# A hybrid decoder layer on one core: one column tile of the merge gates taken out of the block products, and the order of splits, weight rounding and squares changed around the output projection

## The chip, the cores and the metric

The kernel runs on one core of one Trainium2 chip. The metric is the device time of one execution in microseconds (us). Each kernel is executed several times and its time is the median of those executions; one further execution is taken by the hardware profiler, and every row that is read here comes from that one. The engines are named as in the profile: PE is the matrix engine (PEld its weight loads), DVE the vector engine, ACT the scalar engine, POOL the general engine, SP the queue that issues most DMAs.

## What is computed

One layer of a decoder, for 512 tokens of width 1024, in float32. The part that the change touches is the mixer sublayer and the start of the memory sublayer:

```
h    = rms_norm(x) * gain
proj = h @ w_in          # q | k | v | u | B | C | g_a | g_b
o_a  = stick_breaking_attention(q, k, v)          # 8 heads of 64
y_b  = B * causal_conv3(C * u)
merged = sigmoid(g_a) * (o_a @ w_branch_a) + sigmoid(g_b) * (y_b @ w_branch_b)
x    = x + merged @ w_mix_out
x    = x + memory_cross_attention(rms_norm(x), rms_norm(mem), ...)
x    = x + swiglu(rms_norm(x)) ;  out = rms_norm(x)
```

The gates g_a and g_b are 1024 columns each, so eight column tiles of 128 for each of them.

## The kernel before, in words

All activations are held transposed: 128 channels on the partitions, 512 tokens along the free dimension. Every float32 operand of a matmul is **split** into two parts of a shorter float32 format (fp32r): a rounded copy "hi", made by ACT, and the remainder "lo", made by DVE as a subtraction. A product is then three matmuls, hi by hi, hi by lo and lo by hi (`mm3`, lines 170 to 173).

**Plain products.** `load_w` (lines 146 to 168, over `load_hi`) loads 128 columns of a weight (512 KB) into one of four buffers named wr, rounds it on ACT (wh, L163) and subtracts on DVE (wl, L166). `project` and `gemm` make one column tile of h @ w_in from it with 8 x 3 matmuls 512 wide into a PSUM bank of the pool `pmm`, which has two banks (tag mm).

**Block products.** For the wide projections a scheme after Strassen is used: two column tiles and two halves of the tokens form a 2 x 2 block product that needs 7 products in place of 8. `ffn_load` (lines 691 to 710) brings one such pair of column tiles (ws, wg and a22; part of the sums of weights is made by a DMA from POOL that adds into ws, L704), `ffn_raw` and `ffn_form` (lines 708 to 738) make the remaining sums and the splits, and `product` (L747) runs 4 x 3 matmuls 256 wide for each of the 7. The products go to banks z, v and y; v lies in the pool of two banks, z has four banks, y two. `order` (lines 784 to 790) interleaves the 7 products of one pair with those of the next. The gates' pair number m is column tile m of g_a and of g_b.

**Order of the stages around the change.** After the attention, lines 831 to 841 make the gates of the first 3 column tiles by plain products (two of the three were begun within the attention, and one half of the third), squash them with a sigmoid (`squash`), and call `branch` (lines 794 to 804): two gemms of 12 matmuls, first over `yb`, then over `oT`, each followed by a multiplication of its PSUM bank with its gate (L801), and a sum of the two (L803) into one tile of `raw_m`. `gate_pair` reloads x (into wr buffers), scales it and makes the sums that the block products take as their activations (`pair_forms`, `sums_of`, L591 to L595). These lines are ordered by the scheduler of the framework.

Lines 877 to 930 are a **manual schedule**: PE, ACT and DVE each run their instructions exactly in the order in which the program states them; the DMA queues are not part of it. It has two parts. First the last 5 column tiles of the gates as block products, each followed by its `branch` when its seventh product is done; `merge` splits the tiles of `raw_m` into `merged` (L185 on ACT, L186 on DVE) somewhere between them. Then the output projection `mix`, which is `block` inside `residual` (lines 632 to 681): for each of 8 column tiles one gemm of 24 matmuls into a bank of the two-bank pool, then `finish`, which adds x (L659), scales it by the gain of the next norm (xr, L661), splits it and makes the block forms for the memory queries (`even_forms`, `odd_forms`, L601 to L621), squares x (L671 on ACT) and adds the square to a running sum (L674 on DVE). `mix_w(m)` loads and rounds the weight of column tile m two tiles ahead and puts its subtraction on a list, `late`; `catch_up` runs what is on the list. Ahead of the loop `mix_w` is called for tiles 0 and 1, at the products (last_m, 2) and (last_m, 5) of the gates, each time with `catch_up` right behind it. Squares of tiles 0 to 6 are added through `late`, so behind the addition of x of the next tile.

Lines 932 to 954 are the **memory queries**: 4 block pairs, 28 products, with ACT and DVE reading the banks and making the weights' forms six products ahead (`AHEAD`).

Of the kernel before, what the change touches and what calls it, by code (L numbers as in the profile page):

```python
# [9 lines left out]
F32R = mybir.dt.float32r  # L10
AF = mybir.ActivationFunctionType
ALU = mybir.AluOpType

P = 128
# [16 lines left out]
NT = (NF - HOLD - TURN) // 2  # L31
NB = D // (2 * P)
QM = NF + NB
GATES = 5
GM = QM + D // (2 * P)
GATE_AHEAD = 4
MEM_AT = (5, 7, 9, 11)
# [10 lines left out]
def hybrid_layer(ctx: ExitStack, tc: tile.TileContext, xT_d, memT_d, cols_d, wv_d, win_d,  # L48
# [27 lines left out]
    def f(ap):  # L76
        return ap.bitcast(F32)
# [67 lines left out]

    def load_w(src, cols=P):

        w, rest = load_hi(src, cols)
        rest()
        return w  # L150

    def load_hi(src, cols=P):

        k = D // cols
# [5 lines left out]
        hi = wpool.tile([P, k, cols], F32R, tag="wh", name=nm("wh"))  # L160
        lo = wpool.tile([P, k, cols], F32R, tag="wl", name=nm("wl"))
        h2, l2 = (t.rearrange("p k c -> p (k c)") for t in (hi, lo))
        after(nc.scalar.copy(h2, raw), lead[-1:])  # L163

        def rest():
            lows.append(nc.vector.tensor_tensor(out=l2, in0=raw, in1=f(h2), op=ALU.subtract))  # L166

        return (hi, lo), rest
# [458 lines left out]
    def listed(first, oh, ol, ch, cl, dh, dl):  # L627
        a, b = slice(0, HS), slice(HS, S)
        return [first, (oh[:, a], ol[:, a]), (ch[:, a], cl[:, a]), (dh[:, a], dl[:, a]),
                (ch[:, b], cl[:, b]), (dh[:, b], dl[:, b]), (oh[:, b], ol[:, b])]  # L630

    def residual(w_dram, act, old, gain):


        xn = []
        acc = tmp("acc")
        ps, w, even, late = {}, {}, {}, []

        def weight(m):
            w[m], rest = load_hi(w_dram[m])  # L640
            late.append(rest)

        def catch_up():
            while late:
                late.pop(0)()

        def block(m, k0, k1, bank=mmtile):
            if k0 == 0:
                if m not in w:
                    w[m] = load_w(w_dram[m])  # L650
                ps[m] = bank("r")
            for k in range(k0, k1):
                mm3(ps[m], (w[m][0][:, k, :], w[m][1][:, k, :]), act[k], k == 0, k == KD - 1)
            if k1 == KD:
                finish(m)

        def finish(m):
            xm = old[m]
            nc.vector.tensor_tensor(out=xm, in0=ps[m], in1=xm, op=ALU.add)  # L659
            raw = f(unit("xr"))  # L660
            nc.scalar.activation(raw, xm, AF.Copy, scale=gain[:, m:m + 1])  # L661
            catch_up()
            if m % 2:
                xn.append(odd_forms(*even.pop(m - 1), raw))
            else:
                even[m] = even_forms(raw)
            if m == 0:
                nc.scalar.activation(acc, xm, AF.Square)
            else:
                sq = tmp("sq")  # L670
                nc.scalar.activation(sq, xm, AF.Square)  # L671

                def add():
                    nc.vector.tensor_tensor(out=acc, in0=acc, in1=sq, op=ALU.add)  # L674

                if old is x1 and x_loads and m < KD - 1 and not om:
                    late.append(add)
                else:
                    add()

        return (old, xn, acc), block, weight, catch_up

    KP = KD // 2
    SCALED = 3
# [109 lines left out]
    def branch(m, sig, w, also=()):  # L794
        for j, a in ((1, yb), (0, oT)):
            ps = mmtile("br")
            gemm(ps, w, a, 4 * j)
            for g in also[j:j + 1]:
                g()
            with tc.high_priority(100):  # L800
                nc.vector.tensor_tensor(out=sig[j], in0=ps, in1=sig[j], op=ALU.mult)  # L801
# [75 lines left out]
    with tc.manual_schedule(engines={mybir.EngineType.PE, mybir.EngineType.Activation,  # L877
                                     mybir.EngineType.DVE}):
        wb, last_m = {}, GM + GATES - 1

        def merge(n):
            for _ in range(n):
                merged.append(split(raw_m[len(merged)], "m"))

        for n, (m, i) in enumerate(gs):
            product(bank_of(m, i), m, i)
            if i == 1 and m > GM:
                gate_second(m - 1)
            gate_reads(m, i)
            if (m, i) == (last_m, 4):  # L890
                gate_second(m)
            if n + GATE_AHEAD < len(gs):
                ffn_form(*gs[n + GATE_AHEAD])
            if n + GATE_AHEAD + SUM_AHEAD < len(gs):
                ffn_raw(*gs[n + GATE_AHEAD + SUM_AHEAD])
            if i == 3:
                wb[m] = load_w(wbr_d[KD - GATES + m - GM])
            if (m, i) in ((last_m, 2), (last_m, 5)):
                if i == 2:
                    mix_all, mix, mix_w, catch_up = residual(wmix_d, merged, x1, g_q)  # L900
                mix_w(i // 3)
                catch_up()
            if (m, i) == (last_m - 1, 6):
                merge(2)
            if i == 6:
                if m == last_m:
# [4 lines left out]
                branch(KD - GATES + m - GM, (b["g"], b["t"]), wb[m],  # L911
                       (lambda: None, lambda: merge(1)) if m == last_m else ())
                sigmoid = b["sigmoid"]
            if m == last_m and i in (1, 2, 3, 4):
                merge(1)
        merge(KD - len(merged))

        qs = order(QM, MH)
        for m in range(KD):
            mix(m, 0, KD - 1)  # L920
            if m + 2 < KD:
                mix_w(m + 2)
            mix(m, KD - 1, KD)
            for n in {2: range(4), 4: range(4, AHEAD + SUM_AHEAD)}.get(m, ()):
                ffn_raw(*qs[n], nc.gpsimd)
            for n in {5: (0,), 6: (2, 3, 4)}.get(m, ()):
                ffn_form(*qs[n])
        catch_up()
        ffn_form(*qs[5])
        x1, x1f, acc1 = mix_all  # L930

    with tc.manual_schedule(engines={mybir.EngineType.PE, mybir.EngineType.Activation,
                                     mybir.EngineType.DVE}):
        for n, (m, i) in enumerate(qs[:3] + [(QM + 1, 0)]):
            product(bank_of(m, i), m, i, range(KP - 1 - n // 3))
        for m, i in qs[:3]:
            product(bank_of(m, i, False), m, i, range(KP - 1, KP))
        mks = [mem_load(k2) for k2 in range(KD // 2)]
        for n, (m, i) in enumerate(qs):
            if (m, i) == (QM + 1, 0):  # L940
                product(bank_of(m, i, False), m, i, range(KP - 2, KP))
            elif n > 2:
                product(bank_of(m, i), m, i)
            if i == 1 and m > QM:
                second(m - 1)
            elif (m, i) == (QM + MH - 1, 5):
                second(m)
            reads(m, i)
# [424 lines left out]
```

## Time and profile before

| | before |
|---|---|
| median of the runs | 858.8 us (855.7, 858.8, 859.72) |
| profiled execution, its time | 857.22 us |
| span of its instructions | 855.3 us (1.9 us lie outside the span) |
| busy, PE / PEld / DVE / ACT / POOL | 842.0 / 763.4 / 675.7 / 484.6 / 84.1 us |
| mean granted PE clock | 0.997 |

A row of the timeline has the start in us from the span's start, the duration, the engine, the line of the kernel, the operation, the tile written and the tiles read, the shapes, a count, and in brackets the idle time of the engine just before it with what ended it. Matmuls are pipelined: each lasts longer than the distance to the next, so their pace is read from start to start. The view of waits gives, for each engine and line, what it waited for, the total in us, the number of times and the longest. The view of windows gives busy time of each engine in a stretch of the span, and the clock that PE was granted in it.

### The profile page before, as it was taken

To read this page: it belongs to the slowest core of one execution; us is meant where nothing else is said; L and a number is where in the kernel's file an instruction comes from. 1 tells how busy PE (TensorE), PEld (TensorE's weight loads), DVE (VectorE), ACT (ScalarE), POOL (GpSimd) and SP (SyncE) were. 2 spreads that over 40 slices of the span, in tenths; PEclk is the share of its full clock that TensorE was granted. 3 is DMA by queue.
4 is the path that set the end of the run, shared out by engine and by line. 5 is a ranking of instruction groups with operands and counts; after the bars stand their busy time and mean duration, and the time that the engine had idled before them with its cause. 6 is when DMAs were issued, how large, how long until landed. Compare 5 with 4: busy or idle time off the path is not lost.

```text
span 855.3 us, 14081 instructions
## 1 busy us (share of the span) xinstructions
PE 842.0 (98%) x5380; PEld 763.4 (89%) x5380; DVE 675.7 (79%) x1179; ACT 484.6 (57%) x873; POOL 84.1 (10%) x107
## 2 busy tenths in 40 slices
PE   9999999999999989999999999999999999999997
PEld 7878787888899978899988889999999999888997
DVE  9769889987866857878865789888888878966864
ACT  7556766676544535667654666555554456652345
POOL 1011112211010010000000011111111110010002
PEclk9999999999999999999999999999999999999999
DMA  8432232216583664466433437777767775462312
GB/s 296 129 118 79 95 104 80 90 50 199 158 194 102 234 152 108 133 157 226 136 100 98 104 82 173 196 186 188 181 175 184 188 192 171 133 153 65 97 42 99
DMA packets 51027, 120.76 MB, mean 141 GB/s; under 512 B 5136, under 2 KB 9232, under 8 KB 50960
## 3 DMA queue, kind: packets, MB, share of 16 engines
q1 hardware_dynamic: 41152, 101.23, 36.3%
q0 software_dynamic: 9520, 18.35, 13.1%
q8 instruction: 42, 0.69, 0.3%
q10 hardware_dynamic: 288, 0.29, 0.1%
q14 instruction: 25, 0.20, 0.1%
HBM read 116.68 MB, written 2.10 MB: 139 GB/s over the span
## 4 chain that ended last, share of the span: by engine, by line
PE 91%; DVE 3%; ACT 2%; DMA 2%; issue 1%; POOL 0%; DVEq 0%; ACTq 0%; POOLq 0%
PE z L747 23%; PE y L747 11%; PE v L747 6%; PE pr L171 5%; PE pr L172 5%; PE pr L173 5%; PE f L172 3%; PE f L173 3%; PE f L171 3%; PE r L171 3%; PE r L173 3%; PE r L172 3%; PE v L277 3%; PE z L449 1%; PE o L477 1%; DMA ws<-in_w_gates_dram 1%
## 5 line engine op out<-in xcount | busy, mean ns | idle before, releaser
L166 DVE TENSOR_TENSOR wl<-wr,wh 128x1024 fp32r<-128x1024 f32 x80 | 97.5, 1222 | 23.9 <-ACT wh L163 21.4
L163 ACT CAST wh<-wr 128x1024 fp32r<-128x1024 f32 x80 | 83.5, 1048 | 54.7 <-PE pr L172 12.0
L747 PE MATMUL z<-xdh,wf 128*128 128x256 f32 x560 | 110.9, 282 | 0.9 <-ACT sa L771 0.9
L747 PEld LDWEIGHTS z<-xdh,wf 128*128 128x128 f32 x560 | 91.0, 189 | 1.3 <-issue 1.1
L171 PE MATMUL pr<-xgh,wh 128*128 128x512 f32 x208 | 81.5, 392 | 0.0
L172 PE MATMUL pr<-xgl,wh 128*128 128x512 f32 x208 | 81.2, 390 | 0.0
L173 PE MATMUL pr<-xgh,wl 128*128 128x512 f32 x208 | 81.1, 390 | 0.0
L747 PE MATMUL z<-xdl,wf 128*128 128x256 f32 x280 | 78.8, 281 | 0.0
L738 DVE TENSOR_TENSOR wf<-s,wf 128x512 fp32r<-128x512 f32 x70 | 48.2, 689 | 27.2 <-ACT wf L737 26.2
L771 ACT COPY sa<-z 128x256 f32<-128x256 f32 x52 | 19.3, 372 | 82.4 <-PE z L747 82.3
L729 DVE TENSOR_TENSOR wf<-wg,wf 128x1024 fp32r<-128x1024 f32 x35 | 42.9, 1224 | 23.2 <-ACT wf L728 23.2
L737 ACT CAST wf<-s 128x512 fp32r<-128x512 f32 x70 | 43.6, 623 | 26.2 <-DVE s L715 16.7
L747 PE MATMUL z<-xch,wf 128*128 128x256 f32 x280 | 56.2, 283 | 0.0
L747 PE MATMUL y<-xch,wf 128*128 128x256 f32 x280 | 56.1, 282 | 0.0
L704 POOL DMA_DIRECT2D ws<-in_w_ffn_in_dram x22 | 26.5, 1203 | 300.4 <-DMA ws<-in_w_ffn_in_dram 156.8
L747 PEld LDWEIGHTS z<-xdl,wf 128*128 128x128 f32 x280 | 53.0, 189 | 0.2
L738 DVE TENSOR_TENSOR wf<-ws,wf 128x512 fp32r<-128x512 f32 x70 | 48.7, 695 | 2.6 <-ACT wf L737 2.4
L737 ACT CAST wf<-ws 128x512 fp32r<-128x512 f32 x70 | 43.0, 617 | 11.1 <-PE v L747 4.6
L171 PE MATMUL f<-acth,wh 128*128 128x512 f32 (+1 forms) x144 | 49.3, 342 | 0.0
L172 PE MATMUL f<-actl,wh 128*128 128x512 f32 (+1 forms) x144 | 49.2, 342 | 0.0
L173 PE MATMUL f<-acth,wl 128*128 128x512 f32 (+1 forms) x144 | 49.2, 342 | 0.0
L747 PE MATMUL v<-xoh,wf 128*128 128x256 f32 x240 | 48.6, 283 | 0.2 <-ACT xoh L611 0.2
(331 smaller groups left out, 2456.3 us busy)
## 6 DMA issues: line engine op xcount, KB each, us to landing
wr<-in_w_in_dram SPq DMA_DIRECT2D x26, 512.0 KB, 3.6
ws<-in_w_ffn_in_dram SPq DMA_DIRECT2D x22, 512.0 KB, 4.1
ws<-in_w_ffn_in_dram POOLq DMA_DIRECT2D x22, 512.0 KB, 5.8
wg<-in_w_ffn_in_dram SPq DMA_DIRECT2D x22, 512.0 KB, 4.5
wr<-in_w_ffn_out_dram SPq DMA_DIRECT2D x14, 512.0 KB, 3.5
a<-in_w_ffn_in_dram SPq DMA_DIRECT2D x22, 256.0 KB, 4.9
wr<-in_w_branch_dram SPq DMA_DIRECT2D x8, 512.0 KB, 3.7
wr<-in_w_mix_out_dram SPq DMA_DIRECT2D x8, 512.0 KB, 4.0
```

Source lines behind the costliest of these rows:

```text
L163: after(nc.scalar.copy(h2, raw), lead[-1:])
L166: lows.append(nc.vector.tensor_tensor(out=l2, in0=raw, in1=f(h2), op=ALU.subtract))
L171: nc.tensor.matmul(ps, a[0], b[0], start=start, stop=False, **kw)
L172: nc.tensor.matmul(ps, a[0], b[1], start=False, stop=False, **kw)
L173: nc.tensor.matmul(ps, a[1], b[0], start=False, stop=stop, **kw)
L277: nc.tensor.matmul(vps[t], xg[k][a][:, sl], wv[k][b], start=k == 0 and (a, b) == (0, 0), stop=k == KD - 1 and a == 1)
L704: nc.gpsimd.dma_start(s13, a[:, 0:4:3, :], accum_op=ALU.add)
L729: nc.vector.tensor_tensor(out=lo, in0=pair, in1=f(hi), op=ALU.subtract)
L737: nc.scalar.copy(hi, raw)
L738: nc.vector.tensor_tensor(out=lo, in0=raw, in1=f(hi), op=ALU.subtract)
L747: nc.tensor.matmul(ps[:, :HS], a, b, start=i < 3 and k == 0 and j == 0, stop=k == KP - 1 and j == 2, skip_group_check=True)
L771: nc.scalar.copy((s[:, :HS], None, None, s[:, HS:], t[:, :HS], t[:, :HS])[i], z)
```

## The change

1. `GATES` goes from 5 to 4: column tile 3 of both gates is made by plain products and its branch runs in the first loop (now 4 rounds, with the four `gate_pair` calls one in each); the block products of the gates are 4 pairs.
2. `load_hi` is cut into `load_raw` (the DMA) and `halves` (rounding, and the subtraction as a function to call later). Ahead of `mix`, tile 0's weight is rounded where it was, but its subtraction now waits until (last_m - 1, 6), behind the products of the last but one tile and ahead of its branch. Tile 1's weight is only loaded at (last_m, 5); it is rounded within the last branch, behind that branch's second multiplication, and subtracted when all merges are done.
3. In `branch` the multiplication L801 now stands ahead of the extra work `also`. The two merges that stood ahead of the last but one branch stand behind its two multiplications; the merge inside the last branch stands behind that branch's first multiplication.
4. In `residual`, squares of tiles 0 to 3 of the output projection stay as they were. Squares of tiles 4 to 7, with their additions, are put on a list `sums` and run after products 6, 9, 12 and 15 of the memory queries. The second user of `residual` (`om` not empty) squares and adds at once, as before.

```diff
-GATES = 5
+GATES = 4
...
-    def load_hi(src, cols=P):
+    def load_raw(src):
         raw = wpool.tile([P, D], F32, tag="wr", name=nm("wr"))
         i = nc.sync.dma_start(raw, src)
...
+        return raw
+
+    def halves(raw, k=KD):
+        hi, lo = (wpool.tile([P, k, D // k], F32R, tag=t, name=nm(t)) for t in ("wh", "wl"))
...
         def weight(m):
-            w[m], rest = load_hi(w_dram[m])
+            if m not in raw:
+                weight_raw(m)
+            w[m], rest = halves(raw.pop(m))
             late.append(rest)
...
-                if old is x1 and x_loads and m < KD - 1 and not om:
+                if m < LATE_SQUARES and not om:
                     late.append(add)
                 else:
                     add()
+            if m < LATE_SQUARES or om:
+                square()
+            else:
+                sums.append(square)
...
             gemm(ps, w, a, 4 * j)
+            with tc.high_priority(100):
+                nc.vector.tensor_tensor(out=sig[j], in0=ps, in1=sig[j], op=ALU.mult)
             for g in also[j:j + 1]:
                 g()
-            with tc.high_priority(100):
-                nc.vector.tensor_tensor(out=sig[j], in0=ps, in1=sig[j], op=ALU.mult)
...
-            if (m, i) in ((last_m, 2), (last_m, 5)):
-                if i == 2:
-                    mix_all, mix, mix_w, catch_up = residual(wmix_d, merged, x1, g_q)
-                mix_w(i // 3)
-                catch_up()
-            if (m, i) == (last_m - 1, 6):
-                merge(2)
+            if (m, i) == (last_m, 2):
+                mix_all, mix, mix_w, mix_raw, catch_up, sums = residual(wmix_d, merged, x1, g_q)
+                mix_w(0)
+            elif (m, i) == (last_m, 5):
+                mix_raw(1)
             if i == 6:
+                also = ()
+                if m == last_m - 1:
+                    catch_up()
+                    also = lambda: merge(1), lambda: merge(1)
+                elif m == last_m:
+                    also = lambda: mix_w(1), lambda: merge(1)
...
-                       (lambda: None, lambda: merge(1)) if m == last_m else ())
+                branch(KD - GATES + m - GM, (b["g"], b["t"]), wb[m], also)
...
         merge(KD - len(merged))
+        catch_up()
...
             if i == 6:
                 mem_split(mks[m - QM], m - QM)
+            if n in (6, 9, 12, 15):
+                sums.pop(0)()
```

`branch` runs its gemm over `yb` first, so `also[1]` runs behind the first multiplication and `also[0]` behind the second.

More of the change, by code (lines that the diff above doesn't have):

```diff
@@ L146, in load_w @@
     def load_w(src, cols=P):
-        w, rest = load_hi(src, cols)
+        w, rest = halves(load_raw(src), D // cols)
         rest()
         return w
-    def load_hi(src, cols=P):
-        k = D // cols
+    def load_raw(src):
         raw = wpool.tile([P, D], F32, tag="wr", name=nm("wr"))
@@ L159, in load_hi @@
             chained(i)
-        hi = wpool.tile([P, k, cols], F32R, tag="wh", name=nm("wh"))
-        lo = wpool.tile([P, k, cols], F32R, tag="wl", name=nm("wl"))
+        return raw
+    def halves(raw, k=KD):
+        hi, lo = (wpool.tile([P, k, D // k], F32R, tag=t, name=nm(t)) for t in ("wh", "wl"))
         h2, l2 = (t.rearrange("p k c -> p (k c)") for t in (hi, lo))
@@ L630, in listed @@
                 (ch[:, b], cl[:, b]), (dh[:, b], dl[:, b]), (oh[:, b], ol[:, b])]
+    LATE_SQUARES = 4
     def residual(w_dram, act, old, gain):
@@ L636, in residual, with weight_raw @@
         acc = tmp("acc")
-        ps, w, even, late = {}, {}, {}, []
+        ps, w, even, raw, late, sums = {}, {}, {}, {}, [], []
+        def weight_raw(m):
+            raw[m] = load_raw(w_dram[m])
         def weight(m):
-            w[m], rest = load_hi(w_dram[m])
+            if m not in raw:
+                weight_raw(m)
+            w[m], rest = halves(raw.pop(m))
             late.append(rest)
@@ L659, in finish, with square @@
             nc.vector.tensor_tensor(out=xm, in0=ps[m], in1=xm, op=ALU.add)
-            raw = f(unit("xr"))
-            nc.scalar.activation(raw, xm, AF.Copy, scale=gain[:, m:m + 1])
+            xr = f(unit("xr"))
+            nc.scalar.activation(xr, xm, AF.Copy, scale=gain[:, m:m + 1])
             catch_up()
             if m % 2:
-                xn.append(odd_forms(*even.pop(m - 1), raw))
+                xn.append(odd_forms(*even.pop(m - 1), xr))
             else:
[L666 to L669, printed above, removed]
+                even[m] = even_forms(xr)
+            def square():
+                if m == 0:
+                    nc.scalar.activation(acc, xm, AF.Square)
+                    return
                 sq = tmp("sq")
@@ L679, in finish @@
                     add()
-        return (old, xn, acc), block, weight, catch_up
+            if m < LATE_SQUARES or om:
+                square()
+            else:
+                sums.append(square)
+        return (old, xn, acc), block, weight, weight_raw, catch_up, sums
     KP = KD // 2
@@ L897, in hybrid_layer @@
                 wb[m] = load_w(wbr_d[KD - GATES + m - GM])
-            if (m, i) in ((last_m, 2), (last_m, 5)):
-                if i == 2:
-                    mix_all, mix, mix_w, catch_up = residual(wmix_d, merged, x1, g_q)
-                mix_w(i // 3)
-                catch_up()
-            if (m, i) == (last_m - 1, 6):
-                merge(2)
-            if i == 6:
-                if m == last_m:
+            if (m, i) == (last_m, 2):
[3 more added lines that the diff above has]
+                mix_raw(1)
+            if i == 6:
+                also = ()
[4 more added lines that the diff above has]
+                    also = lambda: mix_w(1), lambda: merge(1)
                     for k in range(KD):
@@ L910, in hybrid_layer @@
                 b = banks.pop(m)
-                branch(KD - GATES + m - GM, (b["g"], b["t"]), wb[m],
-                       (lambda: None, lambda: merge(1)) if m == last_m else ())
+                branch(KD - GATES + m - GM, (b["g"], b["t"]), wb[m], also)
                 sigmoid = b["sigmoid"]
```

## The prediction, on record before the result

> **What bounds the kernel now.** I read the page first, for the busy shares.
>
> ```profile
> span 855.3 us, 14081 instructions
> PE 842.0 (98%) x5380; PEld 763.4 (89%) x5380; DVE 675.7 (79%) x1179; ACT 484.6 (57%) x873; POOL 84.1 (10%) x107
> ```
>
> PE sets the time. So an edit can do two things only: change the work of PE, or remove or add a stretch in which PE stands or runs slowly. The view of waits lists nearly all such stretches (the one left out is the start):
>
> ```profile
> PE r L171 <- DVE sb L801: 2.7, 1, 2.7
> PE z L747 <- ACT sa L771: 0.9, 1, 0.9
> PE br L171 <- DVE g L323: 0.7, 1, 0.7
> PE v L747 <- DVE xol L616: 0.4, 1, 0.4
> PE y L747 <- DVE xcl L620: 0.3, 1, 0.3
> PE br L171 <- DVE sb L801: 0.3, 1, 0.3
> PE v L747 <- ACT xoh L611: 0.2, 1, 0.2
> PE v L747 <- DVE g L801: 0.2, 1, 0.2
> PE br L172 <- DVE ol L186: 0.2, 1, 0.2
> ```
>
> All nine lie between 203 and 357 us, where the change is made. There are three places: the end of the plain gates (g L323, g L801, ol), the start of the output projection (r, and br <- sb), and the start of the memory queries (xoh, xol, xcl, sa). I read each in the timeline, from start to start.
>
> Output projection, PE:
>
> ```profile
> 294.69 0.28 PE L747 MATMUL y<-xgh,wf 128*128 128x256 f32 x1
> 295.24 0.50 PE L171 MATMUL br<-yh,wh 128*128 128x512 f32 x1 [0.27 <-DVE sb L801]
> 300.59 0.39 PE L173 MATMUL br<-oh,wl 128*128 128x512 f32 x1
> 303.65 0.50 PE L171 MATMUL r<-mh,wh 128*128 128x512 f32 x1 [2.67 <-DVE sb L801]
> 307.63 0.40 PE L172 MATMUL r<-ml,wh 128*128 128x512 f32 x1
> ```
>
> ```profile
> 303.60:307.50 3.90, 3.85 (x10) 3.06 (x11) 1.98 (x3) 1.57 (x2) 1.85 (x2) 0.57 0.75 202
> ```
>
> The last column but two of the window is the granted clock: 0.57. So behind the wait PE ran at about half its clock. For the loss I need the pace of an undisturbed matmul:
>
> ```profile
> 210.16 0.39 PE L171 MATMUL pr<-xgh,wh 128*128 128x512 f32 x1
> 215.60 0.39 PE L171 MATMUL br<-yh,wh 128*128 128x512 f32 x1
> 242.60 4.31 PE z L747 x36
> ```
>
> The first two are the first matmul of a column tile and the first one behind its 24: 5.44 us, 0.227 each at 512 columns. The third, a piece of the chain, gives 4.31 / 36 = 0.120 at 256 columns. The loss here: 295.24 - 294.69 - 0.12 = 0.43; 303.65 - 300.59 - 0.23 = 2.83; and ten matmuls from 303.65 to 307.63 take 3.98 in place of 2.27, 1.71. Together **5.0 us**.
>
> **Part by part.** *The gates of tile 3.* Leaving: 84 matmuls of 256, 84 x 0.120 = 10.06. Coming: 48 of 512, 48 x 0.2267 = 10.88. PE gets **0.8 us** more; its branch is unchanged. The pair's sums and roundings on ACT, DVE and POOL and its DMAs leave as well; PE waits for none of the kind between 224 and 294, so that is worth nothing there.
>
> [...]
>
> *The output projection.* PE waited for L801, which frees the bank. DVE's order shows why it was late:
>
> ```profile
> 283.36 1.22 DVE L166 TENSOR_TENSOR wl<-wr,wh 128x1024 fp32r<-128x1024 f32 x1
> 291.39 0.69 DVE L864 TENSOR_TENSOR fg<-fg,r0b 128x512 f32<-128x512 f32 x1
> 293.29 1.30 DVE L186 TENSOR_TENSOR ml<-m,mh 128x512 fp32r<-128x512 f32 x2 [1.21 <-ACT mh L185]
> 294.50 0.68 DVE L801 TENSOR_TENSOR sb<-br,sb 128x512 f32<-128x512 f32 x1
> 296.43 0.42 DVE L859 SCALAR_TENSOR_TENSOR sb<-z,r0b 128x256 f32<-128x256 f32 x1
> 298.81 1.23 DVE L166 TENSOR_TENSOR wl<-wr,wh 128x1024 fp32r<-128x1024 f32 x1 [1.64 <-ACT wh L163]
> 302.30 0.69 DVE L186 TENSOR_TENSOR ml<-m,mh 128x512 fp32r<-128x512 f32 x1 [1.20 <-ACT mh L185]
> 302.91 0.68 DVE L801 TENSOR_TENSOR sb<-br,sb 128x512 f32<-128x512 f32 x1
> ```
>
> DVE's instructions overlap a little: a 512-wide one takes 0.60 from start to start, a 1024-wide one 1.14. I walk the new order with these. The subtraction at 283.36 leaves; what follows moves up by 1.14, of which a wait for ACT takes back some 0.3, so L864 stands at 290.6. Behind it comes that subtraction (291.2), then L801 at 292.3 in place of 294.50: PE, which wants this bank at 294.81, no longer waits. Split, L801, split and L803 at 0.60 each end at 295.3, so the next tile's L859 starts 1.1 earlier than 296.43. The subtraction at 298.81 with its wait of 1.64 is gone, 2.8. The split at 302.30 with its wait of 1.20 now stands behind L801, 1.8. DVE is ready for the last sb at 302.91 - 1.1 - 2.8 - 1.8 = 297.2; the bank is full at 294.81 + 12 x 0.227 + 0.4, about 297.9. So L801 runs to 298.6 and PE wants the bank at 294.81 + 24 x 0.227 = 300.3. It has 1.7 us to spare, and the **5.0 us** go, the slow clock with them.
>
> What is late next: L801 of the second bank at 300.6, L803, the last split on ACT and DVE to about 303.3, the moved subtraction to 304.5. PE wants that split at about 305.2 (eighth block) and tile 1's weight at 305.7 + 0.45. Both fit, by 1.2 us at the least. Without that cover the subtraction would cost what it is late, at most its 1.2. The DMA of tile 1's weight is issued where it was. Its buffer comes free at 305.7 and not at 300.0 (298.81 + 1.23), so the load that takes it next on SP's queue, and what is queued behind that, may come up to 5.7 us later; I count that as nothing, since tile 2's weight and x are only wanted with tiles 2 and 0, and cover it in the range.
>
> [...] The row shows 0.57 behind an idle gap of 2.67. [...]
>
> *The squares.* ACT squares x, and at the start of the queries PE waits for the forms of tile 7:
>
> ```profile
> 343.19 0.63 ACT L671 ACTIVATE sq<-x 128x512 f32<-128x512 f32 x1
> 347.72 0.63 ACT L671 ACTIVATE sq<-x 128x512 f32<-128x512 f32 x1
> 355.23 0.63 ACT L671 ACTIVATE sq<-x 128x512 f32<-128x512 f32 x1
> 352.16 1.24 PE L747 MATMUL z<-xf,wf 128*128 128x256 f32 x9
> 356.73 0.36 PE L747 MATMUL z<-xdh,wf 128*128 128x256 f32 x1 [0.90 <-ACT sa L771]
> ```
>
> Undisturbed, the matmul at 356.73 would start 15 x 0.12 behind 352.16, at 353.96: 2.8 us lost. The squares at 343.19 and 347.72 each hold up a rounding of weights on ACT (0.53 from start to start) for which DVE waits ahead of L659 of the next tile. Both gone, tile 7's forms come 1.05 earlier. The square at 355.23 stands between them and the read of the bank (L771) that ended the last wait: 0.53 more. So the matmul starts at 355.1, and **1.6 us** go; the rest, 1.2, stays.
>
> The four squares and additions come back among the queries, 0.53 of ACT and 0.60 of DVE each, one in three products (3 x 1.44 us). There DVE was not the bound: PE has no wait from 357 on, and forms are made six products ahead. I take nothing for it; without that cover four late reads would cost up to 4 x 0.53 = 2.1.
>
> *The end of the plain gates.* The waits of 0.7, 0.2 and 0.2 cost 0.89, 0.39 and 0.38 with their slower first matmul.
>
> ```profile
> 206.05 0.37 SPq L699 DMA_DIRECT2D ws<-in_w_gates_dram  x1
> 211.59 8.65 DMA ws<-in_w_gates_dram
> 214.66 0.42 DVE L595 SCALAR_TENSOR_TENSOR c<-c,xp 128x256 f32<-128x256 f32 x1
> 217.33 1.23 DVE L729 TENSOR_TENSOR wf<-wg,wf 128x1024 fp32r<-128x1024 f32 x1 [1.64 <-ACT wf L728]
> 218.47 0.68 DVE L323 TENSOR_TENSOR g<-pr,r0b 128x512 f32<-128x512 f32 x1
> 223.74 0.42 DVE L595 SCALAR_TENSOR_TENSOR c<-c,xp 128x256 f32<-128x256 f32 x1
> ```
>
> ```profile
> wr<-in_w_in_dram SPq DMA_DIRECT2D x26, 512.0 KB, 3.6
> ```
>
> L323 frees a bank and stood behind L729, a form for the block products whose weight had come late. L323 could have run once its bank was full, at about 215.9. Now block products begin 10.88 + 5.44 = 16.3 us of PE later, so their forms should no longer press in; the tile adds to DVE three subtractions, two L323 and three of the branch, 3 x 1.14 + 5 x 0.60 = 6.4 us in 16.3. Bounds: at best all three waits go, 1.7; at worst the two weights added to four buffers come late (rival A). I take **0.9**, nearest to the row of L323; the wait for ol is untouched.
>
> **Sum**, from the profiled execution (855.3 of span and 1.9 around it): 857.2 + 0.8 - 5.0 - 1.6 - 0.9 = 850.5. The median of the runs is 1.6 above that execution, by which it would be 852.1; I predict the middle, **851.3**.
>
> **The rivals.** A: *the added weights come late.* They, and the branch's, pass through four buffers that x's forms set free (L595 is the last reader of an x). If the second added weight got the buffer of the last x, freed at 224.2, it would be ready at 224.2 + 3.6 for the load + 2 x 1.2 for rounding and subtraction = 230.2. PE wants it at 215.60 + 5.44 for a branch + 5.44 for the first added half = 226.5: 3.7 lost, and 1.7 for the clock: 856.7. [...] Against: the earlier buffers come free sooner, one for the issue at 206.05, the third at 215.1, and from there the weight would be ready at 221.1.
>
> B, the slower one: *the first block weight comes late.* From the issue at 206.05 to ws complete (211.59 + 8.65) and split are 16.4 us. The added work moves the start of the block products to 221.0 + 16.3 = 237.3, and PE wants ws in their third, at 237.3 + 2 x 1.44 = 240.2, so it decides from an issue later than 224. Issued with the fourth branch (232), PE stands 8 us, with the block products (237.3) 13.5; with the middle, 10.8, and 1.7 for the clock: 863.8. Against: PE gives it 16 us more.
>
> C: *the projection's wait stays*, because another instruction of DVE or the last split is what r then waits for: 851.3 + 5.0 = 856.3. Against: 1.7 us to spare.
>
> D: *the slow clock stays* although the gap goes: 851.3 + 1.7 = 853.0.
>
> **How the numbers follow.** Forecast 0.64, A 0.14, B 0.10, C 0.08, D 0.04. A measurement of this kernel tells about 0.5%, 4.3 us, from no change. Faster by more: forecast and D, 0.68; within: A and C, 0.22; slower: B, 0.10. The forecast's own range: down by the 0.8 left at the gates' end, the 1.2 left at the queries and the lowest run (3 below the median), up by 2.1 for squares and 1.2 for the subtraction: 846.5 to 855. To hold 8 in 10 it takes in A and C: 846.5 to 858.
>
> **What would show it.** Right: no wait of r for sb, clock 1.00 throughout 290 to 320, z's wait for sa at about half, 48 more plain matmuls and 84 fewer block ones, no square of tiles 4 to 7 on ACT ahead of the queries. Wrong: a new wait of PE on wh, wl or wf between 215 and 245, or r waiting for ml or wl, or tile 0's addition waiting for its x.

## The result and the profile after

| | before | after |
|---|---|---|
| median of the runs | 859.26 us (855.70 to 861.44, 6 runs) | 850.38 us (849.12 to 852.01, 6 runs) |
| ratio, with its 95% interval | | 0.9902 [0.9877, 0.9927] |
| profiled execution, its time | 857.22 us | 851.58 us |
| span | 855.3 us | 849.5 us |

The change is faster by 1.0%. The forecast was 851.3 us in the median, and 850.5 worked out from the profiled execution; that execution now took 851.58, so this sum was 1.1 us too low.

The page of the kernel after, its busy line, and the view of PE's waits (what waited, for whom, total us, times, longest):

```profile
span 849.5 us, 13985 instructions
PE 839.6 (99%) x5344; PEld 760.7 (90%) x5344; DVE 671.7 (79%) x1169; ACT 479.9 (56%) x866; POOL 82.7 (10%) x106
```

```profile
PE warm L236 <- DVE neg L94: 1.6, 1, 1.6
PE pr L171 <- DVE g L813: 1.6, 1, 1.6
PE z L761 <- ACT sa L785: 0.4, 1, 0.4
PE y L761 <- DVE xcl L620: 0.3, 1, 0.3
PE br L172 <- DVE ol L186: 0.2, 1, 0.2
```

L813 is the multiplication in `branch` that was L801, L761 the block product that was L747, and L785 the reading of its bank. PE has 36 matmuls fewer (84 gone, 48 come). The wait of r for sb, 2.7 us, is gone; that of z for sa is 0.4 in place of 0.9. And there is a wait that was not there: pr, a plain gate's bank, 1.6 us. The first row is the start of the kernel, the same before and after.

The start of the output projection, in the timeline of PE, and the same stretch in the view of windows (last column but two: granted clock):

```profile
295.61 0.28 PE L761 MATMUL y<-xgh,wf 128*128 128x256 f32 x1
295.73 0.40 PE L171 MATMUL br<-yh,wh 128*128 128x512 f32 x1
...
300.97 0.39 PE L173 MATMUL br<-oh,wl 128*128 128x512 f32 x1
301.19 0.39 PE L171 MATMUL r<-mh,wh 128*128 128x512 f32 x1
```

```profile
303.00:307.00 4.00, 4.00 (x19) 3.33 (x18) 1.99 (x3) 1.47 (x2) 0.04 (x1) 1.00 0.57 215
```

From start to start 0.12 and 0.22: nothing is lost, and the clock is 1.00. Why, is seen in DVE's timeline:

```profile
293.53 1.22 DVE L166 TENSOR_TENSOR wl<-wr,wh 128x1024 fp32r<-128x1024 f32 x1
294.66 0.69 DVE L813 TENSOR_TENSOR sb<-br,sb 128x512 f32<-128x512 f32 x1
...
299.39 0.68 DVE L813 TENSOR_TENSOR sb<-br,sb 128x512 f32<-128x512 f32 x1
300.69 0.69 DVE L186 TENSOR_TENSOR ml<-m,mh 128x512 fp32r<-128x512 f32 x1 [0.61 <-ACT mh L185]
...
303.55 0.69 DVE L186 TENSOR_TENSOR ml<-m,mh 128x512 fp32r<-128x512 f32 x1 [0.74 <-ACT mh L185]
304.16 1.22 DVE L166 TENSOR_TENSOR wl<-wr,wh 128x1024 fp32r<-128x1024 f32 x1
```

The last sb ends at 300.07, 1.1 us ahead of PE's 301.19; the forecast had 1.7 to spare. The first ends at 295.35 for PE's 295.73, only 0.4 ahead, where the walk had it 1.8 ahead (292.3 + 0.69 against 294.81).

The start of the memory queries, PE and then ACT:

```profile
347.94 1.24 PE L761 MATMUL z<-xf,wf 128*128 128x256 f32 x9
...
350.12 0.38 PE L761 MATMUL y<-xcl,wf 128*128 128x256 f32 x1 [0.32 <-DVE xcl L620]
...
351.01 0.36 PE L761 MATMUL z<-xdh,wf 128*128 128x256 f32 x1 [0.38 <-ACT sa L785]
```

```profile
350.02 0.62 ACT L751 CAST wf<-ws 128x512 fp32r<-128x512 f32 x1
350.55 0.36 ACT L785 COPY sa<-z 128x256 f32<-128x256 f32 x1
```

The last z starts 3.07 behind the first row, where 15 x 0.12 = 1.80 would be undisturbed: 1.3 lost in place of 2.8. Of it, 0.5 is a rounding of weights that stands ahead of the bank's copy on ACT.

The new wait, in the timeline of all engines:

```profile
208.73 1.05 ACT L163 CAST wh<-wr 128x1024 fp32r<-128x1024 f32 x1 [3.56 <-DMA wr<-in_w_in_dram]
...
209.71 0.39 PE L173 MATMUL br<-oh,wl 128*128 128x512 f32 x1
209.81 1.23 DVE L166 TENSOR_TENSOR wl<-wr,wh 128x1024 fp32r<-128x1024 f32 x1 [2.83 <-ACT wh L163]
...
210.95 0.69 DVE L813 TENSOR_TENSOR g<-br,g 128x512 f32<-128x512 f32 x1
...
211.69 0.50 PE L171 MATMUL pr<-xgh,wh 128*128 128x512 f32 x1 [1.60 <-DVE g L813]
```

The weight is that of the first added gate; PE doesn't need it yet. But its subtraction stands on DVE ahead of the multiplication that frees PE's next bank. DVE stood 2.83 us for a weight that came late, with the multiplication queued behind it. From start to start PE lost 211.69 - 209.71 - 0.227 = 1.75.

### The profile page after: what moved, and what is told of

Read it like the earlier page. It is cut to its first block, busy times and chain, and to the rows that moved or that the text cites. A ratio compares the mean times of both kernels' runs of the same rounds, so it can differ in the third digit from the quotient of the medians.

```text
span 849.5 us, 13985 instructions
## 1 busy us (share of the span) xinstructions
PE 839.6 (99%) x5344; PEld 760.7 (90%) x5344; DVE 671.7 (79%) x1169; ACT 479.9 (56%) x866; POOL 82.7 (10%) x106
## 4 chain that ended last, share of the span: by engine, by line
PE 94%; DVE 2%; ACT 1%; DMA 1%; issue 0%; POOL 0%; DVEq 0%; ACTq 0%; POOLq 0%
PE z L761 23%; PE y L761 11%; PE pr L171 6%; PE pr L172 6%; PE pr L173 6%; PE v L761 6%; PE f L171 3%; PE f L172 3%; PE f L173 3%; PE r L172 3%; PE r L173 3%; PE r L171 3%; PE v L277 3%; PE z L449 1%; PE br L171 1%; PE br L172 1%
## 5 line engine op out<-in xcount | busy, mean ns | idle before, releaser
L166 DVE TENSOR_TENSOR wl<-wr,wh 128x1024 fp32r<-128x1024 f32 x82 | 100.9, 1234 | 22.1 <-ACT wh L163 21.6
L761 PE MATMUL z<-xdh,wf 128*128 128x256 f32 x544 | 107.7, 282 | 0.4 <-ACT sa L785 0.4
L171 PE MATMUL pr<-xgh,wh 128*128 128x512 f32 x224 | 87.8, 392 | 1.6 <-DVE g L813 1.6
L761 PEld LDWEIGHTS z<-xdh,wf 128*128 128x128 f32 x544 | 88.4, 189 | 0.7 <-issue 0.6
L172 PE MATMUL pr<-xgl,wh 128*128 128x512 f32 x224 | 87.4, 390 | 0.0
L173 PE MATMUL pr<-xgh,wl 128*128 128x512 f32 x224 | 87.4, 390 | 0.0
L761 PE MATMUL z<-xdl,wf 128*128 128x256 f32 x272 | 76.6, 281 | 0.0
L785 ACT COPY sa<-z 128x256 f32<-128x256 f32 x52 | 19.4, 372 | 81.9 <-PE z L761 81.8
L761 PE MATMUL z<-xch,wf 128*128 128x256 f32 x272 | 54.6, 283 | 0.0
L761 PE MATMUL y<-xch,wf 128*128 128x256 f32 x272 | 54.5, 282 | 0.0
L171 PEld LDWEIGHTS pr<-xgh,wh 128*128 128x128 f32 x224 | 42.1, 188 | 10.6 <-DVE g L813 2.0
L761 PEld LDWEIGHTS z<-xdl,wf 128*128 128x128 f32 x272 | 51.4, 189 | 0.2
L173 PEld LDWEIGHTS pr<-xgh,wl 128*128 128x128 f32 x224 | 42.0, 188 | 8.9
L172 PEld LDWEIGHTS pr<-xgl,wh 128*128 128x128 f32 x224 | 42.1, 188 | 8.3
```

Of the source, the lines that this page charges most:

```text
L171: nc.tensor.matmul(ps, a[0], b[0], start=start, stop=False, **kw)
L172: nc.tensor.matmul(ps, a[0], b[1], start=False, stop=False, **kw)
L173: nc.tensor.matmul(ps, a[1], b[0], start=False, stop=stop, **kw)
L761: nc.tensor.matmul(ps[:, :HS], a, b, start=i < 3 and k == 0 and j == 0, stop=k == KP - 1 and j == 2, skip_group_check=True)
L785: nc.scalar.copy((s[:, :HS], None, None, s[:, HS:], t[:, :HS], t[:, :HS])[i], z)
```

## The experiments

The theory: the reordering takes away the projection's wait (up to 5.0 us with the slow clock behind it), the moved squares 1.6, and the fourth plain tile pays 0.8 for what it removes at the end of the plain gates. Each run below names the kernel that it starts from. Ratios are against runs of the kernel before on the same chip.

**The kernel before, unaltered.**

> The kernel before, unchanged, to see how its executions spread. The medians differ by 8.9 us, the profiled executions by 5.6 us only. Theory V: executions of before differ in how many stretches of 3.4 us at half clock they hold (1.7 us each), so slower executions show a lower mean clock, by 0.002 for each 1.7 us. Rival: executions differ by something that both kernels share (after spreads over 2.9 us), and the mean clock doesn't go with the time. Both expect a median of 857 to 860 and, in the profile, r waiting 2.7 us for sb.

Measured: 857.02 us (855.30 to 862.09, 10 runs); the shared runs of before 856.93 (854.41 to 863.07, 25 runs), ratio 1.0002 [0.9977, 1.0026]. The kernel spreads over 8 us, and its median was 856.9, 857.2, 858.1 and 859.3 us on four occasions, so the gain in medians depends on the occasion: 8.9 us in the result above, 6.8 on the other occasion on which both kernels ran (last experiment). Neither theory V nor its rival holds alone. Executions of this kernel with a mean clock of 0.999 had spans of 852.5 to 853.9 us, those with 0.997 of 853.4 to 858.8, those with less of 856.4 to 862.7. So the slower clock goes with the time, but at one and the same mean clock over 5 us of spread remain, and their cause stays open. In the profiled execution, span 854.5, PE waited 2.7 for r again, and the windows behind show the slow clock:

```profile
303.00:305.00 2.00, 1.91 (x5) 1.54 (x6) 1.33 (x3) 0.55 (x2) 0.57 (x1) 0.50 0.85 293
305.00:307.00 2.00, 2.00 (x8) 1.64 (x7) 0.69 (x1) 1.02 (x2) 1.04 (x2) 0.76 0.51 98
```

A stretch of 3.4 us, as in theory V, stands in the first profile of this kernel: its clock was 1.00 up to 304.1 and again from 307.6, and between them 0.50:

```profile
304.20:307.50 3.30, 3.30 (x9) 2.57 (x8) 1.39 (x2) 1.57 (x2) 1.85 (x2) 0.50 0.70 173
```

**The order alone** (from the changed kernel).

```diff
-GATES = 4
+GATES = 5
```

> The changed kernel with five block pairs of gates as before (GATES = 5), so only the order of splits, weights and squares is changed. Theory (the order removes the wait of r): no wait of r, clock 1.00 there, PE has 0.8 us less work than after, and the plain gates end as before (waits of 0.7, 0.2, 0.2 and 1.97 us lost, in place of the new wait of 1.6 and 2.37 lost): 1.2 us faster than after, 849.2. Rival (one block pair less is what relieves DVE): r waits for sb again, 2 us or more with the slow clock behind it, 854 to 855.

Measured: 853.02 us (849.79 to 857.46, 10 runs), ratio 0.9950 [0.9927, 0.9973]; profiled span 848.5, no wait of r, clock 1.00 from 303 to 307. So the order takes the wait away without the fourth tile. At the end of the plain gates v waits 0.6 us. The median is 3.8 us above the theory's 849.2: four executions took 849.8 to 851.4 us, six 852.2 to 857.5. The slow clock doesn't account for the second group, since all but its longest execution have mean clocks of 0.998 to 1.000, as the first group has 0.998 and 0.999.

**The fourth tile alone** (from the kernel before).

```diff
-GATES = 5
+GATES = 4
```

> The kernel before with GATES = 4 and nothing else. Theory: the wait of r for sb stays at 2.7 us with the clock at about 0.57 behind it, the new wait of pr for g (1.6 us) is there, PE has 0.8 us more: 1.2 us slower than before, 860.5. Rival (one pair less relieves DVE): the wait of r is gone or below 1 us, 854 to 855.

Measured: 856.78 us (854.87 to 857.92, 10 runs), ratio 0.9997 [0.9979, 1.0015]: worth nothing, where 1.2 us more had been expected. The wait of r is there in full, but this time without the slow clock:

```profile
PE r L171 <- DVE sb L801: 2.7, 1, 2.7
```

```profile
303.00:305.00 2.00, 1.74 (x8) 1.44 (x9) 1.49 (x3) 0.39 (x1) 0.07 (x1) 1.00 0.91 341
305.00:307.00 2.00, 2.00 (x10) 1.67 (x9) 0.69 (x1) 1.19 (x2) 1.93 (x2) 1.00 0.24 64
```

Also in this execution no wait of pr, though DVE's order there is the same as in the changed kernel; the table further down shows what differs. At the start of the last branch br waits 0.9 us for sb, where the kernel before waited 0.3.

**The squares put back** (from the changed kernel).

```diff
-                if m < LATE_SQUARES and not om:
+                if m < KD - 1 and not om:
...
-            if m < LATE_SQUARES or om:
-                square()
-            else:
-                sums.append(square)
+            square()
...
-            if n in (6, 9, 12, 15):
-                sums.pop(0)()
```

> The changed kernel with all squares in the output projection, as before. Theory: the waits of the first queries are those of before (xoh 0.2, xol 0.4, xcl 0.3, sa 0.9; 2.8 us lost from the undisturbed start of z<-xdh, 1.2 in after), 1.6 us slower than after in the span, about 851.1. Rival (something else shortened these waits, the earlier start of the projection for one): waits as in after, span 849.5.

Measured: one execution, 852.32 us, span 850.3, so the time alone settles little. The loss at the start of the queries is 2.8 again, z waiting 0.9 for sa as before. It is 2.8 in all four profiles with the squares in place (two of the kernel before, the fourth tile alone, this one) and 1.3 in both of the changed kernel: the squares are 1.5 of it.

What sets the rest shows on ACT in the changed kernel. The rounding of the last projection weight (tile 7) waits for its DMA, and xr of tile 5 stands right behind it, ahead of all of ACT's later work towards the forms of tile 7:

```profile
334.54 1.05 ACT L163 CAST wh<-wr 128x1024 fp32r<-128x1024 f32 x1 [4.05 <-DMA wr<-in_w_mix_out_dram]
335.49 0.72 ACT L668 ACTIVATE xr<-x,gcol 128x512 f32<-128x512 f32 x1
```

With the squares moved, the loss at the queries follows this wait nearly us for us: 1.15 us at a wait of 3.95 (weights back), 1.27 at 4.05, 1.82 at 4.62 (the order alone), 2.33 at 5.12 (splits back). So the rest is again a late weight with other work queued behind it. No run moved this rounding, so what that would gain is not shown.

**The weights put back** (from the changed kernel).

```diff
                 mix_all, mix, mix_w, mix_raw, catch_up, sums = residual(wmix_d, merged, x1, g_q)
                 mix_w(0)
+                catch_up()
             elif (m, i) == (last_m, 5):
-                mix_raw(1)
+                mix_w(1)
+                catch_up()
...
-                    also = lambda: mix_w(1), lambda: merge(1)
+                    also = lambda: None, lambda: merge(1)
```

> The changed kernel with the output projection's weight work put back where it was before: both weights rounded and subtracted during the last blocks (tile 0 at the third-last, tile 1 at the sixth piece of the last tile), nothing beside the last branch; the splits stay behind the multiplications and the squares among the queries. Theory (the order of the last splits is what removes the wait of r): the last branch's L801 and L813 no longer stand behind a split, the last sb is ready at about 299.6 to 300.2 where TensorE wants its bank at about 300.3, so at most 0.3 us is lost at the start of the projection, and the time is within 0.5 us of the changed kernel's (about 850.5). Rival (the moved weight is the main cause): the wait of r comes back with at least 1.4 us, and in some executions a stretch at half clock behind it, so 852 to 855.

Measured: 850.82 us (850.60 to 851.86, 4 runs), ratio 0.9915 [0.9887, 0.9943]. The median is the forecast one, but the forecast of the wait was wrong: r waits 1.2, and from start to start 1.37 are lost. Waits, then DVE:

```profile
PE r L171 <- DVE sb L813: 1.2, 1, 1.2
```

```profile
298.44 1.23 DVE L166 TENSOR_TENSOR wl<-wr,wh 128x1024 fp32r<-128x1024 f32 x1 [1.64 <-ACT wh L163]
...
300.64 0.68 DVE L813 TENSOR_TENSOR sb<-br,sb 128x512 f32<-128x512 f32 x1
```

The subtraction and its wait stand ahead of the reading of the last gate's bank and so of sb, as they did before.

**The splits put back ahead** (from the changed kernel).

```diff
             gemm(ps, w, a, 4 * j)
-            with tc.high_priority(100):
-                nc.vector.tensor_tensor(out=sig[j], in0=ps, in1=sig[j], op=ALU.mult)
             for g in also[j:j + 1]:
                 g()
+            with tc.high_priority(100):
+                nc.vector.tensor_tensor(out=sig[j], in0=ps, in1=sig[j], op=ALU.mult)
```

> The changed kernel with the splits put back ahead of the multiplications in the last two branches; the second projection weight stays beside the last branch and the squares among the queries. Theory (either half of the order change suffices for most of it): the last sb is ready at about 299.1 to 299.8, no wait of r, 0 to 0.2 us lost, time within 0.5 us of the changed kernel's. Rival (the order of the splits is the main cause): the wait of r comes back with at least 1 us, so 852 or more. If this run and its counterpart with the weights back both show no wait, the two edits are each enough alone and the gain is not their sum.

Measured: 851.51 us (851.15 to 853.35, 5 runs), ratio 0.9924 [0.9894, 0.9953]. r waits 0.4 (0.55 from start to start), and br at the start of the last branch 0.3 (0.45). DVE in this stretch (L815 is the multiplication here):

```profile
299.19 0.69 DVE L186 TENSOR_TENSOR ml<-m,mh 128x512 fp32r<-128x512 f32 x1 [1.21 <-ACT mh L185]
299.80 0.68 DVE L815 TENSOR_TENSOR sb<-br,sb 128x512 f32<-128x512 f32 x1
```

The median is about 1.1 us above the changed kernel's, where at most 0.5 had been expected. The profiled execution, the longest of the five, also had a slow clock at the start of the queries, where four stands of 0.3 to 0.4 us lost 2.3 us (last column but two):

```profile
351.50:355.00 3.50, 3.45 (x17) 3.48 (x18) 3.22 (x6) 1.50 (x4) 0.00 (x0) 0.53 0.47 123
```

The two halves together explain the 2.83: weights back costs 1.37, splits back 0.55, both 2.83 (the kernel before). The two losses don't add up to the third, because 1.1 us are to spare when neither is there (the changed kernel). By an estimate from these numbers the weights delay sb by 1.1 + 1.37 = 2.5 and the splits by 1.1 + 0.55 = 1.7; both together, less the 1.1 to spare, would lose 3.1, near the 2.83. My walks were too early for both kernels. For the weights the rival's wait (1.4) is nearer to what came than mine (0.3); for the splits the wait lies between (0.2 and 1). So the moved weight is the larger part, but each move alone takes away at least half.

**The multiplication first** (from the changed kernel).

```diff
-        w = load_w(win_d[col // P])
+        w = load_w(win_d[col // P]); len(muls) == 6 and after(lows[-1], muls[2:3])
...
-                nc.vector.tensor_tensor(out=sig[j], in0=ps, in1=sig[j], op=ALU.mult)
+                muls.append(nc.vector.tensor_tensor(out=sig[j], in0=ps, in1=sig[j], op=ALU.mult))
...
-        ffn_form(*qs[5])
...
+            if n == 0: ffn_form(*qs[5])
             if n + AHEAD < len(qs):
```

> The changed kernel with two orders altered. On VectorE the subtraction of the first added gate weight comes after the multiplication of branch 1's first bank, where it stood ahead of it and waited 2.83 us for its weight; and at the start of the memory queries the form of the sixth block is made after the first bank's copy, where its rounding stood ahead of that copy. Theory (the new wait of pr is this multiplication held in line behind a late weight; the wait of z is that copy held behind the rounding): the wait of pr, 1.6 us in the profiled execution of the changed kernel, is gone, and the excess of 0.54 us at the first z of the queries falls to under 0.15; the span falls by 1.9 to 2.3 us to about 847.4, the median by 1 to 2.3 us (in some executions of other kernels with the same tiles the wait of pr was shorter), to about 848.5. Rival (the late weight itself holds TensorE: the wait moves on to the first plain gate that needs it, or to the transfers behind the slot that it frees later): the loss of about 1.9 us stays at the end of the plain gates, and only the 0.4 us at the queries is gained.

Measured: 849.61 us (848.79 to 850.06, 6 runs), ratio 0.9898 [0.9875, 0.9921], span 847.7. The waits of PE behind its start, then rows of DVE, ACT and PE:

```profile
PE v L761 <- DVE xol L616: 0.4, 1, 0.4
PE y L761 <- DVE xcl L620: 0.3, 1, 0.3
PE br L172 <- DVE ol L186: 0.2, 1, 0.2
```

```profile
206.99 0.69 DVE L813 TENSOR_TENSOR g<-br,g 128x512 f32<-128x512 f32 x1 [0.44 <-PE br L173]
```

```profile
347.83 0.62 ACT L619 CAST xdh<-c 128x512 fp32r<-128x512 f32 x1 [0.59 <-DVE c L617]
348.36 0.36 ACT L785 COPY sa<-z 128x256 f32<-128x256 f32 x1
```

```profile
209.51 0.39 PE L171 MATMUL pr<-xgh,wh 128*128 128x512 f32 x1
```

The waits of pr and of z are gone: the multiplication now waits for PE's bank alone and starts 2.5 us before PE wants it, at 209.51. But not the whole gain is the order's. In this execution the weight also landed sooner (4.7 us, table below): the weight was rounded at 207.96; by the old order DVE would have subtracted at 208.0 and multiplied from 209.1 to 209.8, so 0.3 us too late for PE's 209.51, and not 1.75. At the queries nothing was gained on the whole: the excess at the first z is 0.08, but v now waits 0.4 for xol, and the loss of the place is 1.46, where the changed kernel lost 1.27. Tile 7's weight came later here, with a wait of 4.72 on ACT; by the figures under the squares that alone would have made the loss an estimated 1.9, so the moved form took about 0.5 off it. The span fell by 1.8 us, a little less than the 1.9 to 2.3 expected, and the median is 1.1 above the expected 848.5. In the median the kernel is 0.8 us under the changed one; the intervals overlap, so that is not settled as a gain.

**Five tiles, and two repetitions.** The kernel of the last experiment with `GATES = 5`, in which only the place of the form at the queries differs from the order alone; the changed kernel itself; the order alone, again.

> The kernel of f1_mult_first with five column tiles of gates as block products, as before the change, in place of four (so the reordered multiplication has no added gate weight to stand ahead of). Theory P (the block product saves what its matmuls save): 84 block matmuls in place of 48 plain ones are 0.8 us less on TensorE, so the time is 0.8 us under that of f1, plus what is lost at the end of the plain gates (0.7 us for v waiting for its multiplication in the one profiled execution seen with the order alone): about equal, 849.0 to 850. Theory Q (the fourth tile of plain gates takes away something that only some executions of the five-tile kernels pay, the two groups of times seen with the order alone, 850 to 851 and about 854): the times spread over 848.5 to 853, the median 1.5 to 3 us over f1's.

> The changed kernel itself, unaltered, beside the two others on the same chip: its median again about 850.4, its executions within 1.5 us of it, and the wait of pr between 1 and 1.7 us in the profiled execution if it comes from the order on VectorE; none or under 0.5 us if it is an accident of one execution.

> The kernel with five column tiles as block products and all the rest of the change, a second time and on the same chip as the changed kernel. Theory P: its median is 0.8 us under the changed kernel's less the waits at the end of the plain gates, so 849 to 851. Theory Q: its executions fall again in two groups some 3.5 us apart, the median 1.5 to 3 us over the changed kernel's; if the profiled execution is one of the slower group, its page shows the place as a wait that the first profile of this kernel (span 848.5 us, 0.6 us for v) doesn't have.

Measured on one chip (before: 857.18 us, 855.16 to 864.63, 12 runs): five tiles 850.02 us (849.35 to 850.93), ratio 0.9914 [0.9895, 0.9932], span 847.9; the changed kernel 850.37 (849.70 to 851.32), 0.9916 [0.9899, 0.9932], span 848.6; the order alone 851.02 (849.93 to 854.43), 0.9931 [0.9910, 0.9952], span 848.7; 6 runs each. With five tiles the wait of pr is not there and the one before the change is:

```profile
PE br L171 <- DVE g L323: 0.7, 1, 0.7
```

In the second profile of the order alone this wait is 1.3 us, and v waits 0.2.

Theory P holds: with four or five tiles the time is the same within what can be measured. Q falls for the first kernel, whose executions lie within 1.6 us. Some executions of the order alone still take 2 to 4 us more than the rest, and none of the profiles is of such an execution; what they wait for stays open. The changed kernel's wait of pr was 1.2 us in its second profile, so it is no accident of one execution, but its size varies. What it varies with shows in these kernels, all with the subtraction ahead of the multiplication on DVE, but for the last row:

| | adding DMA ahead of the load by | load of the added weight | lost at pr |
|---|---|---|---|
| changed | 1.19 us | 6.1 us | 1.75 us |
| changed, again | 1.07 | 5.7 | 1.34 |
| weights back | 1.00 | 5.6 | 1.30 |
| squares back | 1.00 | 5.6 | 1.29 |
| splits back | 0.55 | 4.4 | 0 |
| fourth tile alone | 0.44 | 4.3 | 0 |
| multiplication first | 0.95 | 4.7 | 0 |

The first column is the issue of the weight's load on SP less the issue on POOL of the DMA that adds into ws (202.54 - 201.35 in the first row). The ends of the second column, in the view of DMA issues, for the changed kernel and for the fourth tile alone (KB, then us from issue to landing):

```profile
wr<-in_w_in_dram SPq DMA_DIRECT2D x1, 512.0 KB, 6.1
```

```profile
wr<-in_w_in_dram SPq DMA_DIRECT2D x1, 512.0 KB, 4.3
```

The further the adding DMA is ahead, the longer the load takes, and at 4.4 us and less nothing is lost. The last row shows that this is not all of it: at 0.95 the load took 4.7 us, at 1.00 it took 5.6. That the adding DMA slows the load is the author's estimate from these rows and from the median of the changed kernel's 28 loads of this kind, 3.6 us; no run here took the adding DMA away, so it is argued and not shown.

## Why the prediction was right, and where it was not

| step | forecast | measured in the profiled execution |
|---|---|---|
| gates of tile 3, work of PE | +0.8 | 84 and 48 matmuls, as counted |
| output projection | -5.0 | -5.0: no wait of br or r, clock 1.00 |
| squares | -1.6 | -1.5 (2.77 to 1.27) |
| end of the plain gates | -0.9 | +0.5 (0.89 + 0.39 + 0.38 before; 1.75 + 0.39 after) |
| elsewhere | 0 | -0.6, the rest of the span: 0.26 of it ahead of the wait for ol, the remainder in pieces too small to name |
| sum | -6.7 | -5.8 in the span (-5.6 in the time) |

The 0.89, 0.39 and 0.38 are taken from start to start up to the matmul that waited. The forecast says that its slower first pace is in them; it is not, and adds about 0.1 at each wait, before and after.

**PE as the bound**: right. All but the 0.6 of "elsewhere" is work of PE, or a stretch in which PE stood or was slow.

**The output projection**: right in the mechanism and in the sum. The walk was 0.6 us too early at the last sb and 1.4 at the first. What was late next came as walked: the last split ends at 303.55 + 0.69 = 304.24 and tile 1's subtraction at 305.38. Less the 0.92 by which PE's wish for the first bank moved (295.73 against 294.81), these are the 303.3 and 304.5 of the forecast. The two moves were costed together; apart, the weight is worth more than the splits.

**The slow clock** was taken as a fixed 1.71. It isn't: the same wait of 2.7 us was followed by half clock (0.50) in two profiled executions of the kernel before, and by full clock (1.00) in that of the fourth tile alone. So the change takes 3.3 us there (0.43 + 2.83) when the clock stays full, and 5.0 when it halves.

**The end of the plain gates** is the step that failed: its term was mis-sized by 1.4 us, and in sign. Two of the three old waits went, those for L323 and L801, and the one for ol stayed at 0.39: L323 no longer stands behind a block form. But an added weight took the block form's place, ahead of another multiplication that frees a bank. Rival A had the late weight and the four buffers, but looked for PE waiting on the weight itself; PE waited for the multiplication queued behind its subtraction, and lost 1.75 us. The row of L729 ahead of L323, quoted for the old wait, was the pattern of the new one: the forecast asked whose form goes, and not which late operand moves in.

**The squares** were right in the mechanism and nearly in the size, 1.5 for 1.6. The 1.2 that was to stay did stay, as 1.27; the forecast didn't ask what sets it, and the runs point to the late weight of tile 7. Run among the queries, the squares cost nothing, as taken: PE has no wait behind 351 us. B, C and D didn't happen: no wait for wf, r waits for nothing, the clock is 1.00.

That the median came within 0.9 us is in part luck. The forecast was the middle between two bases; from the profiled execution alone the sum was 1.1 us too low, while the medians of the result fell by 8.9 us, 3.3 more than the profiled executions. The medians of the kernel before moved by 2.4 us between occasions, for reasons that stay open.

## What to carry to other kernels

In a kernel like this one, look at what stands just ahead, on the same engine, of each instruction that frees a bank, and whether it waits for a DMA: here a subtraction that stood 2.83 us for a late weight held the multiplication behind it to 210.95, and PE waited 1.6 us for that, though it didn't need the weight yet. Put the freeing instruction first and the preparation behind it; here that took the wait of 1.75 us away, in an execution in which the old order would still have lost an estimated 0.3. When an edit removes such a neighbour, ask which instruction moves into its place and what that one waits for.

## What the runs showed of the hardware

- Behind a stand of PE of 2.7 us the granted clock was half in two executions and full in a third: 0.50 from 304.2 to 307.5 and 0.50 from 303 to 305 in the two profiles of the kernel before, 1.00 from 303 to 307 in that of the fourth tile alone. Single stands of 1.2 to 1.6 us were followed by no slow stretch in the profiles above: in the changed kernel the clock was 1.00 from 211.6 to 231, behind the 1.6, and the mean clock of the profiles with the others was 0.998 to 1.000. Four stands of 0.3 to 0.4 us, 2.3 us lost within 4, were followed by 0.53 from 351.5 to 355 in the profile with the splits back; in four other profiles the same place lost 2.8 and the clock stayed at 1.00. What decides between the two is not shown.
- A load of 512 KB from SP took 4.3 to 6.1 us beside an adding DMA of the same size from POOL that had been issued 0.44 to 1.19 us ahead of it; 4.3 belongs to 0.44 and 6.1 to 1.19. That the one slows the other is argued, as said above.
